# Floor, squares and head factors of four mLSTM heads: f32 column sums and a spread through memory in place of a weighted sum and diagonals

## The chip, the cores and the metric

The kernel runs on one core of a Trainium2 chip. A core has a matrix engine (TensorE, PE in the profile), three engines for elementwise work (VectorE, DVE; ScalarE, ACT; GpSimd, POOL) and one that issues transfers (SyncE, SP). POOL issues transfers as well. The metric is the device time of one execution in microseconds; a time given for a kernel is the median of its runs.

## The reference

Two layers over 512 tokens with 1024 channels. The first (layer A) mixes tokens by an mLSTM matrix memory with 4 heads of 192 channels beside a cross-attention to 256 memory tokens with 4 heads of 64, the second by a banded attention with 12 heads beside another cross-attention. Each has an output projection and a gated convolutional feed-forward part. What the change touches is the end of an mLSTM head:

```
h  = num / maximum(abs(den), exp(-m))
hm = h * rsqrt(mean(h*h over the 192 channels of the head) + EPS)
mix = hm * a_head_g * sigmoid(o)
```

`num` is the weighted sum of the values, `den` the sum of the weights, `m` the running maximum of the exponents. Since `h` is `num` over a number per token and head, the two steps are one factor per token and head: the product of `num` with `rsqrt(mean(num*num) + EPS * max(den*den, exp(-2m)))`. This is what the kernel computes.

## The kernel before, in words

Activations stand with channels on the 128 partitions and the 512 tokens along the free axis, in tiles of 128x512. A product of two f32 matrices is done by `mm3` (L167 to L171) as three products of a high and a low part: high by high (L169), high by low (L170), low by high (L171). `split` makes the two parts, the high one by a copy on ACT (L130), the low one by a difference on DVE (L131). Weights come by SP's queue into `wr` and are split into `wh` and `wl`.

In layer A the work of PE comes from two sources. A *job*, which is a generator, makes the parts that depend on one another: `mlstm_head(h)` for heads 0 to 3, and `memory_attention` for pairs of memory heads. A *filler* makes matmuls of projections and of the output projection, which wait for little. `weave(job, filler, each)` takes so many units of filler (a unit is one `mm3`) for each step of the job; `yield n` in a job stands for n steps. The order is: head 0, head 1, memory attention 0, head 2, memory attention 1, head 3. Filler for the first four is the input projection of later tiles; for memory attention 1 and head 3 it is the output projection. The order in which instructions come to an engine is then settled by a scheduler that works from the program, except where `pin` keeps an instruction at its place.

A head (`mlstm_head`) makes the weighted scores of four blocks of tokens (exponents are read to all partitions from memory into the tile `bias`, L1029; ACT's Exp at L1155, POOL's mask at L1157, the product at L1166), then multiplies them with the values (`products`), into two tiles `nums`. The first has 128 channels of the head. The second has the other 64 on one half of its partitions, and on the other half the denominator, the same in every row. The end of a head before the change:

- ACT squares both tiles (L1193), and DVE multiplies the numerators by the gate `og` (L1195).
- For each of 4 blocks of 128 tokens two f32 products (L1200, L1201) with the small constant matrix `mcf` give two columns per block: the sum of the squared numerators, and the mean of the squared denominator rows. Behind each block stands a yield of 0.581.
- DVE takes the maximum of the second column and `floor2`, scales it and adds the first column (L1205 to L1207). `rsqrt` (L213 to L222) is done by an integer start and three iterations on 128x4 elements.
- `diagonal` (L224 to L237) splits the factor and multiplies two copies of the identity by it (L231); after a yield of 2.673, `spread` (L240 to L245) multiplies a matrix of ones by the two diagonals (L244), so that each partition holds the factor of every token.
- DVE multiplies the gated numerators by it (L1214) and they are split into `mixes`, the operands of the output projection.

`floor2` is the bound `exp(-2m)`. Its row `mr` (4 heads x 512 tokens) is made in `gate_rows`, transposed in four parts by PE (L1097) into tokens x heads, and passed through Exp (L1099).

`OutProjection.part(g, *ks)` adds the products of input tiles ks to the output tiles of group g: group 0 is output tiles 0 to 2, group 1 is 3 and 4. `finish` makes those output tiles that are in no group (5 to 7 before) with `project`, adds each tile to the residual `xT`, and collects the squares for the next norm.

Of the kernel before, what the change touches and what calls it, by code (L numbers as in the profile page):

```python
# [9 lines left out]
F32 = mybir.dt.float32  # L10
# [3 lines left out]
ALU = mybir.AluOpType  # L14
# [9 lines left out]
AH = 4  # L24
# [31 lines left out]
def trunk(  # L56
# [30 lines left out]
    def sb(tag, shape, dtype=F32):  # L87
        count[0] += 1
        return pool.tile(shape, dtype, tag=tag, name=f"{tag}{count[0]}", bufs=bufs[tag])
# [23 lines left out]
    eps = cpool.tile([P, 1], F32, name="eps")  # L113
    V.memset(eps, EPS)

    mcf = cpool.tile([P, 3, 2], F32, name="mcf")
    V.memset(mcf, 0.0)
    V.memset(mcf[:, 0, 0:1], 1.0)
    V.memset(mcf[:HD, 1, 0:1], 1.0)
    V.memset(mcf[HD:, 1, 1:2], 1.0 / HD)  # L120
    V.memset(mcf[:HD, 2, 1:2], 1.0 / HD)
    V.memset(mcf[HD:, 2, 0:1], 1.0)


    HEADS = (slice(0, HD), slice(HD, P))

    pin = tc.keep_in_program_order
# [32 lines left out]
    def weights(*args):  # L160
        return parts(load(*args))

    def rows(w, c0, n, k0=0, k1=None):
        k1 = k1 if k1 is not None else w.shape[0] // P
        return w[k0 * P : k1 * P, c0 : c0 + n].rearrange("(k p) c -> p k c", p=P)
# [4 lines left out]
        nc.tensor.matmul(o, lh, rl, start=False, stop=False, skip_group_check=more)  # L170
        nc.tensor.matmul(o, ll, rh, start=False, stop=last, skip_group_check=more)  # L171

    def project(w, c0, act, tag="mm"):


        n = len(act)
        wh, wl = weights(rows(w, c0, P), n, P)
        o = ps(tag)
        for k in range(n):
            mm3(o, wh[:, k, :], wl[:, k, :], act[k][0], act[k][1], k == 0, k == n - 1)  # L180
            yield
        return o

    def run(gen):
        while True:
            try:
                next(gen)
            except StopIteration as end:
                return end.value
# [57 lines left out]
    def logarithms():  # L247

        pin(A.preload_act_table_set("natural_log_exp_and_others"))
# [357 lines left out]
    class OutProjection:  # L607
# [18 lines left out]

        def finish(self, gnames):
            logarithms()
            norm = Norm()
            acts = [[] for _ in gnames]  # L630
            for j in range(KT):
                o = self.o[j] if j in self.o else run(project(self.w, j * P, self.mixes))
                V.tensor_add(xT[j], xT[j], o)
                pin(G.dma_start(xspill[j], xT[j]))
                norm.add(xT[j])
                for a, g in zip(acts, gnames):
                    a.append(scaled(xT[j], g[:, j : j + 1]))
            return norm, acts
# [373 lines left out]
    e, u, c, r = (cpool.tile([P, TT, AH], F32, name=f"gate{i}") for i in range(4))  # L1012
    tot = cpool.tile([AH, 16], F32, name="tot")
    acol = cpool.tile([P, TT, AH], F32, name="acol")
    floor2 = cpool.tile([P, TT, AH], F32, name="floor2")
    NEXT = 4
    RO = [0, 512, 896, 1152, 1280]

# [12 lines left out]
    def gate_rows():  # L1031
# [58 lines left out]
            spread_exponents(i)  # L1090
        pin(V.tensor_tensor(out=mr, in0=mr, in1=br, op=ALU.add))
        V.tensor_scalar(mr, mr, -40.0, None, op0=ALU.max)
        yield
        tp = ps("tr")
        for T in range(TT):
            nc.tensor.transpose(tp[:, T * AH : (T + 1) * AH], ar[:, T * P : (T + 1) * P], ident[:AH, :AH])
            nc.tensor.transpose(tp[:, 16 + T * AH : 16 + (T + 1) * AH], mr[:, T * P : (T + 1) * P], ident[:AH, :AH])  # L1097
        pin(V.tensor_copy(acol, tp[:, :16].rearrange("p (t h) -> p t h", t=TT)))
        A.activation(floor2, tp[:, 16:32].rearrange("p (t h) -> p t h", t=TT), AF.Exp, scale=-2.0)  # L1099

    mixes = [None] * KT

# [41 lines left out]
    def mlstm_head(h):  # L1144
# [43 lines left out]
        yield from products(2)  # L1188
        yield from products(3)
        sqs = []  # L1190
        for o, j, r in ((nums[0], full, slice(0, P)), (nums[1], sh, rs)):
            sq = sb("t", [P, S])
            A.activation(sq, o, AF.Square)  # L1193
            sqs.append(sq)
            V.tensor_tensor(out=og[j][r, :], in0=o[r, :], in1=og[j][r, :], op=ALU.mult)  # L1195
        yield
        st = ps("sc")
        for T in range(TT):
            sl = slice(T * P, (T + 1) * P)
            nc.tensor.matmul(st[:, 2 * T : 2 * T + 2], sqs[0][:, sl], mcf[:, 0, :], start=True, stop=False)  # L1200
            nc.tensor.matmul(st[:, 2 * T : 2 * T + 2], sqs[1][:, sl], mcf[:, 1 + odd, :], start=False, stop=True)  # L1201
            yield 0.581
        st = st[:, : 2 * TT].rearrange("p (t c) -> p t c", c=2)
        z, fc = small(), small()
        V.tensor_tensor(out=z, in0=st[:, :, 1], in1=floor2[:, :, h], op=ALU.max)  # L1205
        V.tensor_scalar(z, z, EPS, 1e-35, op0=ALU.mult, op1=ALU.max)
        V.scalar_tensor_tensor(z, st[:, :, 0], 1.0 / DH, z, op0=ALU.mult, op1=ALU.add)  # L1207
        rsqrt(fc, z)
        dg = diagonal(fc)
        yield 2.673  # L1210
        fb = spread(dg, "sc")
        yield
        for j, r in ((full, slice(0, P)), (sh, rs)):
            V.tensor_tensor(out=og[j][r, :], in0=fb[r, :], in1=og[j][r, :], op=ALU.mult)  # L1214
            if mixes[j] is None:
                mixes[j] = sb("u", [P, S], F32R), sb("u", [P, S], F32R)
            split(mixes[j][0][r, :], mixes[j][1][r, :], og[j][r, :])

    outp = OutProjection(a_w_out, mixes, (0, 3, "mm"), (3, 5, "tr"))
    run(value_columns(1))  # L1220
    load_vectors(1)
    load_vectors(2)
# [16 lines left out]
    job = mlstm_head(3)  # L1239
    fill = chain(fill, outp.part(0, 7))  # L1240
    weave(islice(job, 13), fill, 0.85)
    fill = chain(fill, outp.part(1, 0, 1, 2, 6), outp.part(1, 3, 7))
    weave(job, fill, 0.862)
    run(chain(fill, outp.part(0, 4, 5), outp.part(1, 4, 5)))
    norm, (act,) = outp.finish([col["gffn"][:, 0:8]])


# [275 lines left out]
```

## Time and profile before

| | |
|---|---|
| runs | 1195.31, 1196.02, 1194.69 us; median 1195.31 |
| profiled execution | 1195.72 us |
| its span, first to last instruction | 1194.0 us |
| mean granted TensorE clock | 0.999 |
| busy PE, DVE, ACT, POOL | 99%, 81%, 61%, 11% |

The page of the profile gives the busy time of each engine, the clock in 40 slices of the span, the chain of work that ended last, and groups of instructions by line. A row of a timeline is: start in us, duration, engine, line, operation, output tile <- input tiles, shape, and in square brackets the engine's idle time ahead of it with what ended it. In a group, "x32 | 5.8, 251" means 32 records, 5.8 us busy, 251 ns mean. Matmuls overlap, so the price of one is the distance from its start to the next one's start. SPq and POOLq are the queues of transfers that SP and POOL issue.

### The profile page before, as it was taken

The page shows a single profiled execution, that of the slowest core. Times are in us where ns is not written, and L with a number is a line of the kernel's source. Part 1 is how long each engine was busy: PE and PEld are TensorE (multiplying, and loading weights), DVE is VectorE, ACT ScalarE, POOL GpSimd, SP SyncE. Part 2 cuts the span into 40 slices and gives each one's busy share as a digit, 9 for nine tenths or more (in the row PEclk, how much of TensorE's full clock was granted, in tenths as well). Part 3 has the DMA queues.
Part 4 walks back from the last instruction along what each step waited for, and adds up shares of the span by engine and source line. Part 5 has one row for each costly group of instructions (what it writes and reads, how often), then busy time and mean ns, then how long its engine had stood idle before and what let it go on. Part 6 is the DMA issues. An engine that isn't in the chain of part 4 may idle for free.

```text
span 1194.0 us, 18184 instructions
## 1 busy us (share of the span) xinstructions
PE 1183.5 (99%) x6719; PEld 1037.0 (87%) x6719; DVE 961.7 (81%) x1760; ACT 725.2 (61%) x1294; POOL 130.3 (11%) x222
## 2 busy tenths in 40 slices
PE   9999999999999999999999999999999999999997
PEld 9988888888899998999888888888889988999986
DVE  6877788788978888888698888997896888888855
ACT  5648677655656555555576677776565655555545
POOL 1211201010021111111020000101001011011100
PEclk9999999999999999999999999999999999999999
DMA  8645313444265676665464313246336455665551
GB/s 289 212 108 140 84 54 80 152 144 141 88 156 147 156 165 165 154 144 123 142 204 123 89 54 101 69 135 185 111 99 141 116 139 135 142 141 139 119 158 71
DMA packets 200155, 158.61 MB, mean 133 GB/s; under 512 B 8344, under 2 KB 179838, under 8 KB 200066
## 3 DMA queue, kind: packets, MB, share of 16 engines
q1 hardware_dynamic: 183906, 119.74, 34.1%
q0 software_dynamic: 15584, 36.67, 14.9%
q8 instruction: 53, 0.87, 0.3%
q10 hardware_dynamic: 576, 1.05, 0.2%
q14 instruction: 36, 0.29, 0.1%
HBM read 128.89 MB, written 32.46 MB: 135 GB/s over the span
## 4 chain that ended last, share of the span: by engine, by line
PE 92%; ACT 3%; DVE 2%; DMA 1%; SPq 1%; issue 0%; POOL 0%; POOLq 0%; DVEq 0%; ACTq 0%
PE pmm L169 15%; PE pmm L170 15%; PE pmm L171 15%; PE ptr L171 6%; PE ptr L169 6%; PE ptr L170 6%; PE pmm L785 6%; PE psc L171 5%; PE psc L170 5%; PE psc L169 5%; PE pmm L784 3%; PE psc L519 2%; PE ptr L1350 1%; DMA wr<-in_mem_w_kv_dram 1%; PE ptr L1371 1%; PE ptr L1372 1%
## 5 line engine op out<-in xcount | busy, mean ns | idle before, releaser
L169 PE MATMUL pmm<-u,wh 128*128 128x512 f32 (+1 forms) x872 | 309.1, 355 | 0.3 <-ACT u L130 0.2
L170 PE MATMUL pmm<-u,wh 128*128 128x512 f32 (+1 forms) x872 | 306.2, 351 | 0.0
L171 PE MATMUL pmm<-u,wl 128*128 128x512 f32 (+1 forms) x872 | 306.0, 351 | 0.0
L131 DVE TENSOR_TENSOR wl<-wr,wh 128x1024 fp32r<-128x1024 f32 (+3 forms) x172 | 199.8, 1163 | 57.0 <-ACT wh L130 55.0
L130 ACT CAST wh<-wr 128x1024 fp32r<-128x1024 f32 (+3 forms) x172 | 172.4, 1004 | 97.7 <-PE pmm L170 44.5
L171 PEld LDWEIGHTS pmm<-u,wl 128*128 128x128 f32 x872 | 164.5, 189 | 21.1
L169 PEld LDWEIGHTS pmm<-u,wh 128*128 128x128 f32 x872 | 164.5, 189 | 18.5 <-ACT u L130 1.1
L170 PEld LDWEIGHTS pmm<-u,wh 128*128 128x128 f32 x872 | 164.7, 189 | 18.2 <-DVE u L131 0.5
L169 PE MATMUL ptr<-u,wh 128*128 128x512 f32 x272 | 106.7, 392 | 0.0
L171 PE MATMUL ptr<-u,wl 128*128 128x512 f32 x272 | 106.1, 390 | 0.0
L753 POOL DMA_DIRECT2D xspill<-t x64 | 55.6, 869 | 461.1 <-ACT t L752 450.4
L170 PE MATMUL ptr<-u,wh 128*128 128x512 f32 x272 | 105.9, 389 | 0.0
L130 ACT CAST u<-pt 128x512 fp32r<-128x512 f32 x102 | 63.0, 620 | 46.8 <-DVE pt L875 46.7
L131 DVE TENSOR_TENSOR u<-pt,u 128x512 fp32r<-128x512 f32 x102 | 69.9, 688 | 11.2 <-ACT u L130 8.5
L169 PE MATMUL psc<-u,wh 128*128 128x256 f32 (+1 forms) x232 | 76.1, 328 | 0.0
L171 PE MATMUL psc<-u,wl 128*128 128x256 f32 (+1 forms) x232 | 75.9, 327 | 0.0
L170 PE MATMUL psc<-u,wh 128*128 128x256 f32 (+1 forms) x232 | 75.9, 327 | 0.0
L937 ACT ACTIVATE t<-t 128x512 f32<-128x512 f32 x34 | 21.6, 634 | 79.3 <-DVE t L660 79.3
L785 PE MATMUL pmm<-u,u 128*128 128x512 f32 x192 | 69.6, 397 | 0.0
L821 DVE TENSOR_TENSOR t<-t,pmm 128x256 f32<-128x256 f32 x72 | 30.2, 419 | 44.9 <-ACT t L819 44.8
L752 ACT COPY t<-ptr 128x512 f32<-128x512 f32 x64 | 37.4, 585 | 43.1 <-PE ptr L171 43.1
L660 DVE SCALAR_TENSOR_TENSOR t<-t,cols,t 128x511 f32<-128x511 f32 x80 | 59.7, 746 | 3.7 <-ACT t L667 3.7
(300 smaller groups left out, 2673.8 us busy)
## 6 DMA issues: line engine op xcount, KB each, us to landing
wr<-in_ffn_w_up_dram SPq DMA_DIRECT2D x54, 512.0 KB, 4.2
wr<-in_ffn_w_down_dram SPq DMA_DIRECT2D x38, 512.0 KB, 4.1
pt<-in_ffn_w_up_dram SPq DMA_DIRECT2D x34, 512.0 KB, 6.2
xspill<-t POOLq DMA_DIRECT2D x64, 256.0 KB, 5.2
wr<-in_a_w_in_dram SPq DMA_DIRECT2D x20, 512.0 KB, 3.7
xspill<-u POOLq DMA_DIRECT2D x32, 256.0 KB, 2.6
u<-xspill SPq DMA_DIRECT2D x32, 256.0 KB, 5.0
wr<-in_w_kv_dram SPq DMA_DIRECT2D x12, 512.0 KB, 3.7
```

Source lines behind the costliest of these rows:

```text
L130: high = A.copy(hi, src) if on_act else V.tensor_copy(hi, src)
L131: low = V.tensor_tensor(out=lo, in0=src, in1=f(hi), op=ALU.subtract)
L169: nc.tensor.matmul(o, lh, rh, start=first, stop=False, skip_group_check=more)
L170: nc.tensor.matmul(o, lh, rl, start=False, stop=False, skip_group_check=more)
L171: nc.tensor.matmul(o, ll, rh, start=False, stop=last, skip_group_check=more)
L519: nc.tensor.matmul(o, a, b, start=first and i == 0, stop=i == 1)
L660: V.scalar_tensor_tensor(acc[:, n:], src[:, : S - n], self.fw[:, c * FT + j : c * FT + j + 1], acc[:, n:], op0=ALU.mult, op1=ALU.add,)
L752: A.copy(t, o)
L753: G.dma_start(xspill[j], t, accum_op=ALU.add)
L784: nc.tensor.matmul(r[:, :H], w[1][:, k], p[i - 1][:, :H], start=False, stop=False, skip_group_check=True)
L785: nc.tensor.matmul(r, w[0][:, k], p[i - 1], start=False, stop=k == n - 1, skip_group_check=True)
L821: V.tensor_tensor(out=o, in0=o, in1=r[:, H:], op=ALU.add)
```

## The change

The bound becomes a row that is passed through Exp before it leaves its 4 partitions, scaled, and written to memory; from there it is read into two tiles, each holding the bound of two heads on 64 partitions each. In a head the squares of the second tile are bounded on the half with the denominator by one operation, and the two squared tiles are added. One f32 product per block with a column of ones then gives the whole sum (the scale takes account of the fact that the denominator stands in 64 rows). Heads 0 to 2 write the factor to memory and read it back to all partitions by POOL's queue, with a yield of 5.2; head 3 keeps the diagonals, with a yield of 4.2. The output projection gets a third group, output tile 5, and its `finish` loads the weights of the first two tiles left before it starts.

```diff
-    mcf = cpool.tile([P, 3, 2], F32, name="mcf")
...
-    def project(w, c0, act, tag="mm"):
+    def project(w, c0, act, tag="mm", ready=None):
...
-        wh, wl = weights(rows(w, c0, P), n, P)
+        wh, wl = ready or weights(rows(w, c0, P), n, P)
...
             logarithms()
+            rest = [j for j in range(KT) if j not in self.o]
+            ready = {j: weights(rows(self.w, j * P, P), KT, P) for j in rest[:2]}
             norm = Norm()
...
-                o = self.o[j] if j in self.o else run(project(self.w, j * P, self.mixes))
+                o = self.o[j] if j in self.o else run(project(self.w, j * P, self.mixes, ready=ready.get(j)))
...
-    floor2 = cpool.tile([P, TT, AH], F32, name="floor2")
+    floor2 = dram.tile([AH, S], F32, name="floor2")
+    floors = []
+    factors = dram.tile([AH, S], F32, name="factors")
...
+        A.activation(mr, mr, AF.Exp, scale=-2.0)
+        V.tensor_scalar(mr, mr, EPS * DH / HD, 1e-35, op0=ALU.mult, op1=ALU.max)
+        G.dma_start(floor2, mr)
+        for hp in range(2):
+            floors.append(sb("u", [P, S]))
+            for odd, half in enumerate(reversed(HEADS)):
+                row = floor2[2 * hp + odd]
+                src = bass.AP(tensor=row.tensor, offset=row.offset, ap=[[0, HD], [1, S]])
+                G.dma_start(floors[hp][half, :], src)
         yield
         tp = ps("tr")
         for T in range(TT):
             nc.tensor.transpose(tp[:, T * AH : (T + 1) * AH], ar[:, T * P : (T + 1) * P], ident[:AH, :AH])
-            nc.tensor.transpose(tp[:, 16 + T * AH : 16 + (T + 1) * AH], mr[:, T * P : (T + 1) * P], ident[:AH, :AH])
         pin(V.tensor_copy(acol, tp[:, :16].rearrange("p (t h) -> p t h", t=TT)))
-        A.activation(floor2, tp[:, 16:32].rearrange("p (t h) -> p t h", t=TT), AF.Exp, scale=-2.0)
...
         sqs = []
+        for o in reversed(nums):
+            sqs.insert(0, sb("t", [P, S]))
+            A.activation(sqs[0], o, AF.Square)
+        dr = HEADS[1 - odd]
+        V.scalar_tensor_tensor(
+            sqs[1][dr, :], sqs[1][dr, :], EPS * DH / HD, floors[hp][dr, :], op0=ALU.mult, op1=ALU.max
+        )
+        V.tensor_add(sqs[0], sqs[0], sqs[1])
         for o, j, r in ((nums[0], full, slice(0, P)), (nums[1], sh, rs)):
-            sq = sb("t", [P, S])
-            A.activation(sq, o, AF.Square)
-            sqs.append(sq)
             V.tensor_tensor(out=og[j][r, :], in0=o[r, :], in1=og[j][r, :], op=ALU.mult)
         yield
+        yield 3.6
         st = ps("sc")
         for T in range(TT):
-            sl = slice(T * P, (T + 1) * P)
-            nc.tensor.matmul(st[:, 2 * T : 2 * T + 2], sqs[0][:, sl], mcf[:, 0, :], start=True, stop=False)
-            nc.tensor.matmul(st[:, 2 * T : 2 * T + 2], sqs[1][:, sl], mcf[:, 1 + odd, :], start=False, stop=True)
-            yield 0.581
-        st = st[:, : 2 * TT].rearrange("p (t c) -> p t c", c=2)
+            nc.tensor.matmul(st[:, T : T + 1], sqs[0][:, T * P : (T + 1) * P], ones[:, :1], start=True, stop=True)
         z, fc = small(), small()
-        V.tensor_tensor(out=z, in0=st[:, :, 1], in1=floor2[:, :, h], op=ALU.max)
-        V.tensor_scalar(z, z, EPS, 1e-35, op0=ALU.mult, op1=ALU.max)
-        V.scalar_tensor_tensor(z, st[:, :, 0], 1.0 / DH, z, op0=ALU.mult, op1=ALU.add)
+        V.tensor_scalar(z, st[:, :TT], 1.0 / DH, None, op0=ALU.mult)
         rsqrt(fc, z)
-        dg = diagonal(fc)
-        yield 2.673
-        fb = spread(dg, "sc")
-        yield
+        if h < AH - 1:
+            pin(G.dma_start(factors[h].rearrange("(t p) -> p t", p=P), fc))
+            fb = sb("rb", [P, S])
+            pin(G.dma_start(fb, bass.AP(tensor=factors.tensor, offset=factors[h].offset, ap=[[0, P], [1, S]])))
+            yield 5.2
+        else:
+            dg = diagonal(fc)
+            yield 4.2
+            fb = spread(dg, "sc")
+            yield
...
-    outp = OutProjection(a_w_out, mixes, (0, 3, "mm"), (3, 5, "tr"))
+    outp = OutProjection(a_w_out, mixes, (0, 3, "mm"), (3, 5, "tr"), (5, 6, "sc"))
...
-    fill = chain(fill, outp.part(1, 0, 1, 2, 6), outp.part(1, 3, 7))
+    fill = chain(fill, outp.part(2, 0, 1, 2, 3, 6, 7), outp.part(1, 0, 1, 2, 6), outp.part(1, 3, 7))
     weave(job, fill, 0.862)
-    run(chain(fill, outp.part(0, 4, 5), outp.part(1, 4, 5)))
+    run(chain(fill, outp.part(0, 4, 5), outp.part(1, 4, 5), outp.part(2, 4, 5)))
```

In the kernel after the change, lines behind the constants stand 9 lines earlier (L169 to L171 become L160 to L162); the bounding operation is L1197, the addition L1200, the column sums L1207, the write and the read of the factor L1212 and L1214, the multiplication by the factor L1222.

More of the change, by code (lines that the diff above doesn't have):

```diff
@@ L114, in trunk @@
     V.memset(eps, EPS)
-    mcf = cpool.tile([P, 3, 2], F32, name="mcf")
[L117 to L122, printed above, removed]
     HEADS = (slice(0, HD), slice(HD, P))
```

## The prediction, made before the change was run

> **What bounds the kernel now.** I read the page first: the busy line, the granted clock, and the chain of work that ended last.
>
> ```profile
> span 1194.0 us, 18184 instructions
> ...
> PE 1183.5 (99%) x6719; PEld 1037.0 (87%) x6719; DVE 961.7 (81%) x1760; ACT 725.2 (61%) x1294; POOL 130.3 (11%) x222
> ...
> PEclk9999999999999999999999999999999999999999
> ...
> PE 92%; ACT 3%; DVE 2%; DMA 1%; SPq 1%; issue 0%; POOL 0%; POOLq 0%; DVEq 0%; ACTq 0%
> ```
>
> PE is busy for 99% of the span, its clock is never held back, and 92% of the chain is PE. So two things count: how many steps PE has to do, and where it stands still. What DVE, ACT and POOL do is free as long as its result is there when PE comes to the instruction that reads it. PE's price per step I took from the timeline, in an undisturbed stretch of projection:
>
> ```profile
> 164.83 0.40 PE L170 MATMUL pmm<-u,wh 128*128 128x512 f32 x1
> ...
> 170.29 0.39 PE L170 MATMUL pmm<-u,wh 128*128 128x512 f32 x1
> ```
>
> The second row is 24 instructions after the first: 5.46 / 24 = 0.2275 us for a 128x512 product. The 0.39 or 0.40 in a row is the pipelined duration; the step from start to start is what a product costs.
>
> The sum below is made against the profiled execution, 1195.72 us with a span of 1194.0. The median of the runs shown, 1195.31, lies 0.41 lower.
>
> **What is removed: steps of PE.** Sums of squares first. The groups say how many products there are, the timeline of PE in head 3 what they cost.
>
> ```profile
> L1201 PE MATMUL psc<-mcf,t 128*128 128x2 f32 x32 | 5.8, 251 | 0.0
> ```
> ```profile
> 241.49 0.28 PE L1200 MATMUL psc<-mcf,t 128*128 128x2 f32 x2
> ...
> 242.30 0.49 PE L169 MATMUL ptr<-u,wh 128*128 128x512 f32 x1
> 242.62 0.40 PE L170 MATMUL ptr<-u,wh 128*128 128x512 f32 x1
> ```
>
> Each of these f32 products leaves two records, so L1201 has 16 products in the four heads, and L1200 as many. Four of them take 242.30 - 241.49 = 0.81 us, and the full product behind them takes 0.32 instead of 0.23: 0.9 for four, 0.225 each. The new sum has 4 products per head instead of 8, so 16 go: **-3.6**. The new ones have one output column instead of two. Two columns cost as much here as 512 do in the other type, so the price doesn't follow the columns and I keep it; if it halved after all, the 16 that stay would give 1.8 more.
>
> The floor row is no longer transposed (L1097), four products less:
>
> ```profile
> 88.75 0.20 PE L1096 MATMUL ptr<-ident,t 4*128 4x4 f32 x1
> 88.81 0.20 PE L1097 MATMUL ptr<-ident,t 4*128 4x4 f32 x1
> ```
>
> A step of 0.06 each: **-0.25**. And heads 0 to 2 lose two spreading products (L244) each: 6 x 0.2275 = **-1.37**. Together -5.2 us.
>
> PE also stands still at places that the change rewrites. The timeline of PE at head 2's spread, at head 2's memory attention, at head 3's first weighted product, and at head 3's end:
>
> ```profile
> 212.61 0.39 PE L171 MATMUL pmm<-u,wl 128*128 128x512 f32 x1
> 212.91 0.50 PE L244 MATMUL psc<-t,onesr 128*128 128x512 f32 x1
> 213.25 0.40 PE L169 MATMUL pmm<-u,wh 128*128 128x512 f32 x1
> 213.51 0.50 PE L244 MATMUL psc<-t,onesr 128*128 128x512 f32 x1
> 213.85 0.39 PE L170 MATMUL pmm<-u,wh 128*128 128x512 f32 x1
> ```
> ```profile
> 233.04 0.28 PE L170 MATMUL psc<-u,u 128*128 128x128 f32 x1
> 233.47 0.73 PE L169 MATMUL ptr<-pt,u 128*128 128x512 f32 x2 [0.16 <-ACT pt L130]
> 234.04 0.22 PE L171 MATMUL psc<-u,u 128*128 128x128 f32 x1
> 234.35 0.50 PE L170 MATMUL ptr<-pt,u 128*128 128x512 f32 x1
> ```
> ```profile
> 186.66 0.39 PE L169 MATMUL pmm<-u,wh 128*128 128x512 f32 x1
> 187.12 0.73 PE L519 MATMUL psc<-u,u 128*128 128x512 f32 x2
> ```
> ```profile
> 251.75 0.39 PE L171 MATMUL ptr<-u,wl 128*128 128x512 f32 x1
> 252.30 0.73 PE L169 MATMUL pmm<-u,wh 128*128 128x512 f32 x2 [0.16 <-ACT u L130]
> ```
>
> Four steps from 212.61 to 213.85 take 1.24 instead of 0.91: 0.33 of waiting. Against their normal step the rows after 233.04 and 234.04 come 0.3 and 0.2 late, 187.12 comes 0.23 late, 252.30 comes 0.32 late. I count **-1.4** for all of them; what is late in their place is counted anew below. That is -6.6 so far.
>
> **What is added: a round trip through memory.** In heads 0 to 2 POOL writes the factor (512 separate elements of four bytes, L1212 after the change) and then reads it back to all partitions (256 KB, L1214). No row shows a write like this one. The nearest are the DMA view's, of the same queue, and the landing line of the tile "bias":
>
> ```profile
> bias<-exponents POOLq DMA_DIRECT2D x4, 256.0 KB, 3.7
> ...
> exponents<-t POOLq DMA_DIRECT2D x1, 8.0 KB, 2.8
> ...
> exponents<-t POOLq DMA_DIRECT2D x1, 2.0 KB, 1.5
> ```
> ```profile
> DMA to landing us min/median/max: 2.9/3.6/7.7
> ```
>
> Lower end: the 2 KB write, 1.5, and the fastest read, 2.9: 4.4. Upper end: 2.8 and the slowest read, 7.7: 10.5. I take 2.4 for the write (same size as the 1.5, but in far smaller pieces, so towards 2.8) and the median 3.6 for the read: a trip of **6.0**. The Trainium skill ("DMA: Bandwidth & Descriptors", Specifications) says that below 512 B a transfer becomes a read-modify-write; no row here shows writes that short, and if it bites, the long-trip rival below is the case.
>
> What waits for the trip: L1222 (the multiplication by the factor) stands on DVE in program order, and what is queued behind it on DVE waits too; PE waits when it comes to a product that needs any of it.
>
> *Head 2* costs most, because memory attention 1 and then head 3 stand behind it. Before, on DVE:
>
> ```profile
> 207.45 0.16 DVE L1205 TENSOR_TENSOR s<-psc,floor 128x4 f32<-128x4 f32 x1 [1.06 <-PE psc L1201]
> ...
> 212.17 1.29 DVE L231 TENSOR_TENSOR t<-ident,s 128x512 fp32r<-128x512 f32 x2
> 214.05 1.28 DVE L1214 TENSOR_TENSOR u<-psc,u 128x512 f32<-128x512 f32 x2 [0.59 <-PE psc L244]
> ```
>
> The sums end at about 207.2, and PE starts head 3's first weighted product (233.47 above) 26.2 us later. In that stretch PE waited 0.66 (the 0.33 of the spread and the 0.3 before 233.47), and in the changed order it has five 512-wide products less (the two spreads, and three of filler that go elsewhere): 26.2 - 0.66 - 5 x 0.2275 = 24.4 us of work. From L1214 to 233.47 the other chain took 19.4: multiply, split, the query scaling, softmax, transposes, values, head 3's scores, its split. In the changed order one weight split of 0.6 moves ahead of the multiplication and runs during the trip: 18.8. Ahead of it stand the sums' arrival (0.25), the operations up to the factor (from 207.45 to 212.17 before, 4.7 us for 14 small and three longer ones; the changed order has two small ones and one of 0.5 less, so 3.8), the trip 6.0, and 0.1 to start: 0.25 + 3.8 + 6.0 + 0.1 + 18.8 = 29.0. PE therefore waits 29.0 - 24.4 = **+4.6**, and every microsecond of the trip counts in full; the break-even is a trip of 1.4. Part of the wait comes even earlier, because the output projection's filler needs head 2's tile itself.
>
> *Head 1*: seven long DVE operations stand between its small ones, so the factor is ready 5.4 us after the sums; 6.0 for the trip and 5.7 for the multiplications, the split and memory attention 0's first reductions make 17.1, where the changed order gives PE 16.5 us of work: **+0.6**, break-even 5.4.
>
> *Head 0*: factor ready after 3.2, then 6.0, two multiplications and the split of head 1's first weighted scores, which is queued behind them (some 2.4): 11.6 against 11.5 us of work on PE (55 instructions): **+0.1**, break-even 5.9.
>
> **What is hidden.** The floors' own trip (a write and four reads) starts about where the transposes stood (88.75) and is first needed at head 0's sums, a whole head later. The bounding operation and the addition on DVE (some 0.7 us each) and the squares come ahead of the sums, covered by 3.6 more units of filler; without the cover each head would lose 1.4. Head 3 keeps its diagonals, with 4.2 units of filler ahead of the spread instead of 2.7, for the sum's filler stands earlier now; I take **+0.1**. The write and read of head 2 on POOL's queue stand ahead of the clearing of memory attention 1's query tiles, which has 2 us of room. SP's queue gets seven loads more because the weights are cut differently, at a DMA load of some 0.6; they are prefetched, so nothing.
>
> **The end of the output projection.** Three column groups are now done as filler, so two projections (16.4 - 5.5 = 10.9 us) instead of three cover the additions and norm sums of the tiles. PE's total work is the same. DVE's room there, by the view of windows:
>
> ```profile
> 255.40:280.00 24.60, 24.60 (x111) 20.35 (x110) 21.33 (x29) 15.03 (x22) 4.36 (x8) 1.00 0.64 200
> ```
>
> The third figure pair is DVE: 21.33 busy in 24.60, 3.3 us free. Cutting 5.5 of cover could cost up to 2.2; but the weight splits of the first two projections are moved forward out of it. Between 0 and 2.2 I take **+0.3**.
>
> **Sum.** -5.2 - 1.4 + 4.6 + 0.6 + 0.1 + 0.1 + 0.3 = -0.9, so 1194.8 in a profiled execution and **1194.4** as a median. The change saves PE about 6.6 us and hands 5.7 of them back as waiting.
>
> **Rivals.**
>
> *Short trip.* The write is as quick as the 2 KB one and the read near the fastest, 4.65 in all. Then heads 0 and 1 wait for nothing and head 2 waits 3.25: -6.6 + 3.25 + 0.4 = -2.95, 1192.4. For the chain of 18.8 I assumed that all of it is late by the full delay; in the window 218 to 233.5 DVE was idle for part of the time, waiting for PE, and if some 1.8 of such waiting closes up, it is 1190.5. I price the case at 1191.4. For it: the DMA queues are lightly used around the heads, and DVE's rows show idle time. Against: the median of the read is 3.6. The Trainium skill ("DMA: Bandwidth & Descriptors", Anatomy of one DMA, SWDGE path) fits 2.0 us plus bytes over 436e3; as an estimate that is 2.0 for the write and 2.6 for the read, 4.6, and by it this rival's time. The trace's 1.5 for 2 KB and 3.7 for 256 KB differ from it in both directions.
>
> *Long trip: slower than before.* 512 four-byte pieces are slow to write, or the read queues behind other traffic as the 7.7 did. At a trip of 8.0 head 2 waits 6.6, head 1 2.6, head 0 2.1: -6.6 + 11.3 + 0.4 = +5.1, 1200.4. From a trip of 6.3 on the change gains nothing, from 7.1 it is slower by over 0.2%. For it: no row shows such a write. Against: 8 KB in 2.8.
>
> *DVE late in the end of the projection.* With the trip as forecast, between the 2.2 above and the whole 5.5 of lost cover is waited for: 1196.3 to 1199.6, priced at 1197.9.
>
> *It doesn't do what it says*: the one-column products cost more than 0.225, for instance. Weight loads of the same size speak against it, and it would only move the sum within the range.
>
> **How the numbers follow.** Forecast (1192.5 to 1196.5): 0.45. Short trip (1190.4 to 1192.4): 0.35. Long trip: 0.12. DVE late: 0.08. About 0.2%, 2.4 us, is what a measurement of this kernel can tell from no change, so the bounds are 1192.9 and 1197.7. Faster: the short trip and 0.05 of the forecast, 0.40. Slower: the long trip and half of the late DVE, 0.16. The same: what is left, 0.44. The range goes from the short trip's lower end, 1190.5, to 1199.0, about a trip of 7.5; what is left out is half of the long trip and a little below.
>
> **What would show it.** PE has 16 + 6 + 4 products less. In head 2 L1212 and L1214 land 6 us after the last rsqrt step, DVE's multiplication waits for DMA, and PE has waits of 4 to 5 us in sum between the output projection's product with head 2's tile and head 3's first weighted product; under 1 us in sum at heads 0 and 1. If the trip is 4.5 or the wait at head 3 is below 3, the short trip holds; if L1212 alone takes 4 or more, the long one. I would be wrong altogether if the wait showed up in the convolution or the second layer, where no instruction changed, or if PE's step changed.

## The result, and the profile after

| | before | after |
|---|---|---|
| median | 1194.91 us (5 runs, 1194.57 to 1196.02) | 1236.84 us (5 runs, 1233.58 to 1240.21) |
| ratio | | 1.0349, 95% interval 1.0338 to 1.0360 |
| profiled execution, span | 1195.72, 1194.0 | 1240.21, 1238.5 |
| mean granted TensorE clock | 0.999 | 0.981 |

The change makes the kernel 3.5% slower, 44.5 us by the two profiled spans. The forecast was 1194.4, with a range that ended at 1199.0, and a rival for which a long trip through memory made it slower, at 1200.4. The direction of that rival is what came, at eight times its size. The page of the profile after, the lines that answer to those shown of before:

```profile
span 1238.5 us, 18111 instructions
...
PE 1191.0 (96%) x6677; PEld 1040.0 (84%) x6677; DVE 961.6 (78%) x1744; ACT 722.1 (58%) x1293; POOL 136.0 (11%) x233
...
PE   9999796959999999999999999999999999999997
...
PEclk9999888979999999999999999999999999999999
...
PE 82%; DVE 6%; DMA 5%; ACT 4%; issue 3%; POOL 0%; SPq 0%; ACTq 0%; DVEq 0%; POOLq 0%
```

A slice is 31 us. PE's row falls to 7, 6 and 5 in the fifth, seventh and ninth, between 124 and 279 us, and in the same stretch the clock's row, all nines before, falls to 8 and 7. Behind 279 us both are as they were. PE's share of the chain went from 92% to 82%, and what came in is DVE, DMA and ACT. (PE's busy time is larger after, although PE has fewer products: the record of a product is longer at half the clock, 0.63 in place of 0.39 in the rows below.)

The view of waits says where, what PE waited for, how often and how long at most:

```profile
PE pmm L160 <- ACT u L121: 11.4, 1, 11.4
PE psc L510 <- ACT t L567: 10.0, 2, 9.9
PE ptr L161 <- DVE pt L122: 9.9, 1, 9.9
PE ptr L160 <- ACT pt L121: 2.6, 2, 1.9
```

Three waits of ten microseconds, one for each trip, and one of 1.9 in head 0 before any trip. ACT and DVE are named, but they only pass the delay on. The timeline of DVE in head 0 shows whom they wait for:

```profile
153.97 1.28 DVE L1222 TENSOR_TENSOR u<-rb,u 128x512 f32<-128x512 f32 x2 [10.33 <-DMA rb<-factors]
155.18 0.68 DVE L122 TENSOR_TENSOR pt<-t,pt 128x512 fp32r<-128x512 f32 x1
```

DVE stands 10.33 us in front of the multiplication, and head 1's split, queued behind it, is what PE needs. POOL's timeline and the DMA view give the trip's two legs (the last figure of a DMA row is the time from issue to landing):

```profile
136.77 0.79 POOL L1212 DMA_DIRECT2D factors<-s  x1 [4.21 <-DVE s L213]
147.56 0.54 POOL L1214 DMA_DIRECT2D rb<-factors  x1 [10.00 <-DMA factors<-s]
```
```profile
rb<-factors POOLq DMA_DIRECT2D x3, 256.0 KB, 6.4
...
factors<-s POOLq DMA_DIRECT2D x3, 2.0 KB, 9.8
```

The write of 2 KB takes 9.8 us, the read 6.4; I had put 2.4 and 3.6. And behind each wait PE itself is slow, as its timeline in head 1's first products shows:

```profile
145.59 0.39 PE L160 MATMUL ptr<-pt,u 128*128 128x512 f32 x1
155.91 0.79 PE L161 MATMUL ptr<-pt,u 128*128 128x512 f32 x1 [9.93 <-DVE pt L122]
156.50 0.63 PE L162 MATMUL ptr<-pt,u 128*128 128x512 f32 x1
156.93 0.63 PE L160 MATMUL ptr<-pt,u 128*128 128x512 f32 x1
...
161.19 0.45 PE L161 MATMUL pmm<-u,wh 128*128 128x512 f32 x1
161.48 0.40 PE L162 MATMUL pmm<-u,wl 128*128 128x512 f32 x1
```

Before the wait a product takes 0.2275, from 156.50 on 0.427, and at 161.2 the full rate is back. The windows view, over the five stretches at half rate, the first of them and the sum (the column behind POOL is the clock):

```profile
123.60:130.30 6.70, 6.70 (x19) 5.40 (x20) 5.24 (x9) 5.14 (x8) 0.51 (x2) 0.51 0.01 2
...
sum 25.10, PE 25.00 PEld 20.47 DVE 19.89 ACT 18.44 POOL 1.15; mean PE 5.00 PEld 4.09 DVE 3.98 ACT 3.69 POOL 0.23
```

So the 44.5 us divide up. Between starts of products, above the normal step, the trace holds gaps of 10.1, 10.0 and 11.6 at the three trips, 2.05 in head 0 before them, and 1.15 and 1.16 later (in memory attention 1 at 273 us, in the feed-forward part at 362): 36.0 in sum. 25.1 us of work at 0.427 in place of 0.2275 cost 25.1 x (1 - 0.2275 / 0.427) = 11.7. Less the 5.2 of products removed that makes 42.5; the last 2 are smaller waits, the longest 0.84.

### The profile page after: what moved, and what is told of

Same layout as the page of the kernel before. It is cut to its first block, busy times and chain, and to the rows that moved or that the text cites. A ratio compares the mean times of both kernels' runs of the same rounds, so it can differ in the third digit from the quotient of the medians.

```text
span 1238.5 us, 18111 instructions
## 1 busy us (share of the span) xinstructions
PE 1191.0 (96%) x6677; PEld 1040.0 (84%) x6677; DVE 961.6 (78%) x1744; ACT 722.1 (58%) x1293; POOL 136.0 (11%) x233
## 4 chain that ended last, share of the span: by engine, by line
PE 82%; DVE 6%; DMA 5%; ACT 4%; issue 3%; POOL 0%; SPq 0%; ACTq 0%; DVEq 0%; POOLq 0%
PE pmm L160 12%; PE pmm L161 12%; PE pmm L162 12%; PE ptr L161 6%; PE ptr L160 6%; PE ptr L162 6%; PE pmm L778 5%; PE psc L162 5%; PE psc L160 5%; PE psc L161 5%; PE pmm L777 3%; PE psc L510 2%; DMA rb<-factors 2%; PE ptr L1358 1%; DVE wl L122 1%
## 5 line engine op out<-in xcount | busy, mean ns | idle before, releaser
L160 PE MATMUL pmm<-u,wh 128*128 128x512 f32 (+1 forms) x864 | 308.4, 357 | 11.5 <-ACT u L121 11.4
L162 PE MATMUL pmm<-u,wl 128*128 128x512 f32 (+1 forms) x864 | 305.3, 354 | 1.0 <-DVE wl L122 1.0
L122 DVE TENSOR_TENSOR wl<-wr,wh 128x1024 fp32r<-128x1024 f32 (+5 forms) x173 | 199.8, 1157 | 66.2 <-ACT wh L121 64.4
L121 ACT CAST wh<-wr 128x1024 fp32r<-128x1024 f32 (+5 forms) x173 | 172.0, 997 | 104.4 <-PE pmm L161 45.8
L160 PEld LDWEIGHTS pmm<-u,wh 128*128 128x128 f32 x864 | 164.8, 191 | 30.5 <-ACT u L121 12.3
L162 PEld LDWEIGHTS pmm<-u,wl 128*128 128x128 f32 x864 | 164.3, 190 | 22.6 <-DVE wl L122 1.4
L160 PE MATMUL ptr<-u,wh 128*128 128x512 f32 x272 | 106.5, 392 | 0.0
L162 PE MATMUL ptr<-u,wl 128*128 128x512 f32 x272 | 106.1, 390 | 0.0
L160 PE MATMUL psc<-u,wh 128*128 128x256 f32 (+1 forms) x240 | 79.7, 332 | 0.0
L162 PE MATMUL psc<-u,wl 128*128 128x256 f32 (+1 forms) x240 | 79.2, 330 | 0.5 <-DVE wl L122 0.5
L161 PE MATMUL psc<-u,wh 128*128 128x256 f32 (+1 forms) x240 | 79.0, 329 | 0.0
```

The costliest lines, as they stand in the source:

```text
L121: high = A.copy(hi, src) if on_act else V.tensor_copy(hi, src)
L122: low = V.tensor_tensor(out=lo, in0=src, in1=f(hi), op=ALU.subtract)
L160: nc.tensor.matmul(o, lh, rh, start=first, stop=False, skip_group_check=more)
```

## The experiments

The theory after reading the two traces: the write is slow because of its 4-byte pieces, and all the rest follows. The rivals: a trip by this queue is always that slow, or the rest of the change (floors, sums, third group) costs too.

### Without the trip: e1_diag, e10_sums, e9_group

```diff
-        if h < AH - 1:
+        if False:
```

> All four heads spread their factor by diagonals and two products, as head 3 does; all else as in the changed kernel (no write, no read back of factors). Theory (the round trip through memory is the whole loss): the three waits of 10 to 12 us and the half-rate stretches behind them go, what stays is the saving of sums and transposes, 1190 to 1193 us. Rival (the rest of the change, that is the third group of the output projection, the new order and the floors' trip, carries part of the loss): 1200 or more, with a PE wait of over 2 us that stays.

1196.87 us median (10 runs, 1195.15 to 1200.04), ratio to before 1.0011 (1.0000 to 1.0021). In the profiled execution the three waits and all half-rate stretches are gone, so the trips are the loss. But the gain that I expected with them gone isn't there: the time lies between the two ranges. The view of waits names one reason:

```profile
PE ptr L160 <- ACT pt L121: 1.6, 1, 1.6
...
PE psc L235 <- DVE t L222: 0.4, 2, 0.2
```

The first is the one of head 0, at 121 us: a cast of the last weighted scores stands on ACT behind a SiLU, whose chain begins with a weight load that lands late. Gaps above the normal step between 80 and 460 us are 8.1 us here and 3.9 before: 4.2 more, against the 3.85 of PE's steps that this kernel saves (5.2 without the 1.37 of the spreads, which are back).

e10_sums also takes back the third group and the early weights:

```diff
-    outp = OutProjection(a_w_out, mixes, (0, 3, "mm"), (3, 5, "tr"), (5, 6, "sc"))
+    outp = OutProjection(a_w_out, mixes, (0, 3, "mm"), (3, 5, "tr"))
```

> e1_diag without the third group of the output projection and without the early weights: before, with only the new floor row, the added squares and the column sums (and the new yields). Theory (in e1_diag PE's saving of 3.85 us is eaten mainly by a wait of 2 us in head 0, where a late weight load stands ahead of the cast of the last weighted scores, and by smaller waits; all of it from the new order in the first heads): the wait near 121 us stays, and the time is within 1.5 us of e1_diag and of before. Rival (the third group eats the saving, since two projections cover less than three): 1191 to 1193.

1197.48 (9 runs, 1196.28 to 1199.76), ratio 1.0023 (1.0013 to 1.0033). This is 0.6 above e1_diag, as expected, but 2.6 above the kernel before (1194.90 beside it), where at most 1.5 was expected. The wait at 121 us stays, so it belongs to the floors, sums and new yields; no run separates these. e9_group has only the third group and the early weights, put into the kernel before:

> The kernel before with only the third group of the output projection and the early weights of its end. Theory (this part is nearly neutral: PE does the same products, and what the early weights save at the end is given back by two late weight splits there): within 1.5 us of before. Rival (it is a gain of its own that the rest of the change hides): 1191 to 1193.

1194.85 (11 runs), ratio 0.9996 (0.9988 to 1.0005): neutral, as expected, and my term of +0.3 for this part lies within the interval. Its trace has no gap of over 0.25 us between 255 and 460 us, so the late splits of the expectation are not there.

### What is slow about the write: e2_row, e3_16b, e4_sp

e2_row makes the factor a row ahead of the write, e3_16b writes four neighbouring values at once and multiplies in that order, e4_sp changes the queue.

```diff
# e2_row
-            pin(G.dma_start(factors[h].rearrange("(t p) -> p t", p=P), fc))
+            fr = st[:TT, P : 2 * P]
+            nc.tensor.transpose(fr, fc, ident)
+            frs = sb("t", [P, S])[:TT, :P]
+            V.tensor_copy(frs, fr)
+            pin(G.dma_start(factors[h].rearrange("(t p) -> t p", p=P), frs))
# e3_16b (the multiplication's matching views are left out here)
+            pin(G.dma_start(factors[h].rearrange("(p t) -> p t", p=P), fc))
# e4_sp
+            pin(nc.sync.dma_start(factors[h].rearrange("(t p) -> p t", p=P), fc))
```

> The factor is transposed by one product into 4 rows and written as 4 pieces of 512 bytes in place of 512 pieces of 4 bytes; read back as in the changed kernel. Theory (the small pieces are what is slow): the write lands in 1.5 to 2 us in place of 9.8, the trip with the transposition is 6 to 8, and the time comes near the recorded forecast, 1193 to 1200. Rival (a trip by this queue is slow whatever is written): the write stays near 10 us and the time near 1237.

> The factor is written in the order partition, block: 128 pieces of 16 bytes; the multiplication reads the spread row in the matching order. Theory (a price for each piece, one after the other: 9.8 less 1.6 over 512 is 16 ns): 1.6 + 128 x 0.016 = 3.7 us for the write, PE waits of about 2 to 3 us less than half of those of the changed kernel, 1198 to 1208. Rival (a price by bytes or by the queue): write near 10, time near 1237.

> The changed kernel with the write of the factor issued by SP's queue in place of POOL's; the read stays on POOL's. Theory (the write is slow in memory, whoever issues it): it lands after 8 to 10 us, PE waits as in the changed kernel, 1225 to 1245. Rival (POOL's queue is what is slow): the write lands in under 3 us and the time is 1198 to 1206, like e2_row and e3_16b.

The DMA views of the three, in that order:

```profile
rb<-factors POOLq DMA_DIRECT2D x3, 256.0 KB, 3.7
factors<-t POOLq DMA_DIRECT2D x3, 2.0 KB, 1.6
```
```profile
rb<-factors POOLq DMA_DIRECT2D x3, 256.0 KB, 4.5
...
factors<-s POOLq DMA_DIRECT2D x3, 2.0 KB, 1.7
```
```profile
rb<-factors POOLq DMA_DIRECT2D x3, 256.0 KB, 6.4
...
factors<-s SPq DMA_DIRECT2D x3, 2.0 KB, 9.1
```

Times: e2_row 1203.65 (ratio 1.0073, 1.0057 to 1.0089), e3_16b 1201.95 (1.0059, 1.0044 to 1.0074), e4_sp 1232.50 (1.0312, 1.0287 to 1.0338). The same 2 KB by the same queue take 1.6 or 1.7 us when the pieces are larger, and by another queue the small ones take 9.1. So the queue is not the cause; but my price of 16 ns a piece falls too, for 128 pieces of 16 bytes should then have taken 3.7. The read behind the slow write is slow too: 6.4 behind the small pieces, 3.7 and 4.5 behind the large ones. What slows it isn't shown; in head 0 of the changed kernel four reads of exponents and SP's transfers run beside it.

With the write repaired the trip is about what I had put it at, and the waits are nearly what I forecast. Yet the times are 9.3 (e2_row) and 7.6 (e3_16b) above the forecast, and e2_row misses the 1193 to 1200 that I expected. The PE timeline of e3_16b at head 2 shows one reason:

```profile
220.44 0.39 PE L162 MATMUL pmm<-u,wl 128*128 128x512 f32 x1
222.44 0.50 PE L160 MATMUL pmm<-u,wh 128*128 128x512 f32 x1 [1.61 <-ACT u L121]
223.35 0.50 PE L161 MATMUL pmm<-u,wh 128*128 128x512 f32 x1 [0.41 <-DVE u L122]
...
225.71 0.63 PE L162 MATMUL pmm<-u,wl 128*128 128x512 f32 x1
```

Even a wait of 1.8 followed by some shorter ones is followed by half-rate products (0.63 in place of 0.39). The other reason is head 0's 1.8 us, which no trip causes.

### What makes pieces slow: e6_pieces, e7_places, e11_spacing

All three spread by diagonals and write, in heads 0 to 2, something that nothing reads, each head another way: e6_pieces and e7_places as their expectations say, e11_spacing the 512 values of 4 bytes into every second, fourth and eighth element.

```diff
# e11_spacing
+            if h < AH - 1:
+                pin(G.dma_start((by8, by16, by32)[h][:, 0].rearrange("(t p) -> p t", p=P), fc))
```

> Spread by diagonals in all heads, and one write per head that nothing reads: head 0 writes 512 pieces of 4 bytes, each 512 bytes from the next; head 1 writes 256 pieces of 8 bytes side by side; head 2 writes 128 pieces of 4 bytes side by side. In e5_unread 512 pieces of 4 bytes side by side took 8.2 to 9.7 us, in e3_16b 128 pieces of 16 bytes took 1.7 to 2.2, so a price of 16 ns for any piece is out. Theory (small pieces that fall into the same stretch of memory are written one after the other, by how many share it): head 0 under 3 us, head 1 about 4 to 5, head 2 about 3 to 4. Rival (each piece under 16 bytes costs about 16 ns wherever it lies): 9 to 10, 5 to 6, 3 to 4. Second rival (the count of pieces of one transfer, past some 128): 9 to 10, 3 to 6, 1.7.

> Spread by diagonals in all heads, and writes that nothing reads: head 0 copies its factor by four transfers of 128 pieces of 4 bytes to another on-chip tile instead of memory; head 1 writes 512 pieces of 4 bytes, 64 bytes apart; head 2 writes 512 pieces of 4 bytes side by side by SP's queue in place of POOL's. Theory (memory writes small pieces of one stretch one after the other): head 0 under 2.5 us each, head 1 under 4, head 2 8 to 10. Rival (the queue or its making of the pieces is slow): head 0 3 to 4 each, head 1 9 to 10, head 2 under 3.

> Spread by diagonals; each of heads 0 to 2 writes 512 pieces of 4 bytes that nothing reads, 8, 16 and 32 bytes apart. So far: side by side (16 in 64 bytes) 8 to 11 us, 64 bytes apart 2.2, 512 bytes apart 2.3; 8-byte pieces side by side 3.6, 16-byte pieces 1.7. Theory (what counts is how many pieces fall into one stretch of 64 bytes, each waiting for the one before): 8 bytes apart 3.5 to 5, 16 apart 2 to 3, 32 apart 2 to 2.5. Rival (the size of a piece counts, if it isn't alone in a far longer stretch, as 512 bytes): 8 to 10 at 8 and 16 bytes, and still over 4 at 32.

Rows of the DMA views, of e6_pieces (512 bytes apart; pairs; 128 pieces), of e7_places (on chip; 64 bytes apart; SP's queue), of e11_spacing (8, 16, 32 bytes apart):

```profile
apart<-s POOLq DMA_DIRECT2D x1, 2.0 KB, 2.3
...
pairs<-s POOLq DMA_DIRECT2D x1, 2.0 KB, 3.6
...
few<-s POOLq DMA_DIRECT2D x1, 0.5 KB, 7.7
```
```profile
onchip<-s POOLq DMA_DIRECT2D x4, 0.5 KB, 1.9
...
lines<-s POOLq DMA_DIRECT2D x1, 2.0 KB, 2.2
...
factors<-s SPq DMA_DIRECT2D x1, 2.0 KB, 11.0
```
```profile
by<-s POOLq DMA_DIRECT2D x1, 2.0 KB, 3.7
...
by<-s POOLq DMA_DIRECT2D x1, 2.0 KB, 2.3
...
by<-s POOLq DMA_DIRECT2D x1, 2.0 KB, 2.4
```

| pieces | within 64 bytes | us |
|---|---|---|
| 512 of 4 bytes, side by side | 16 | 8.2 to 11.0 |
| 128 of 4 bytes, side by side | 16 | 7.7 |
| 512 of 4 bytes, 8 bytes apart | 8 | 3.7 |
| 256 of 8 bytes, side by side | 8 | 3.6 |
| 512 of 4 bytes, 16 bytes apart | 4 | 2.3 |
| 128 of 16 bytes, side by side | 4 | 1.7 |
| 512 of 4 bytes, 32, 64 or 512 bytes apart | 2, 1, 1 | 2.4, 2.2, 2.3 |
| 4 x 128 of 4 bytes, on chip | | 1.9 each |

Neither the number of pieces nor their size decides, and not the queue: a quarter of the pieces, side by side, take nearly as long as all, and 512 pieces apart from one another take 2.3. What orders the whole table is how closely the pieces lie in memory, steeply above four in 64 bytes. The 64 is a ruler and not a finding: all pieces are evenly spaced, and the distance from the start of one to the next (4 bytes, 8, 16 and more) orders the table as well. The row of 128 pieces is one that I had wrong: my theory and the rivals gave it 1.7 to 4 us. Only the write to memory is slow, not the one on chip. That the memory takes such pieces one after the other is the reading that fits; the runs don't show it inside the memory. The Trainium skill ("DMA: Bandwidth & Descriptors", Specifications) has a read-modify-write below 512 bytes; the runs agree that short pieces can be slow, but not that all are, for 4-byte pieces 16 bytes apart took no more than 2.3.

### What the write does to others: e5_unread

```diff
             dg = diagonal(fc)
+            if h < AH - 1:
+                pin(G.dma_start(factors[h].rearrange("(t p) -> p t", p=P), fc))
```

> Spread by diagonals in all heads as in e1_diag, but heads 0 to 2 also write their factor in 512 pieces of 4 bytes, which nothing reads and nothing waits for but the end. Theory (the write also holds up the transfers of the other queues while it lasts): weight loads issued during the write land in 8 to 14 us instead of 3.7, and the time is 2 to 10 us above e1_diag. Rival (only the trip itself costs): the same as e1_diag within 1 us.

1196.03 (10 runs), ratio 1.0011 (1.0001 to 1.0020), as e1_diag; the rival held. The write did delay others: the DMA view between 212 and 235 us has eight reads of "xspill" beside it, first in this kernel, then in the one before.

```profile
u<-xspill SPq DMA_DIRECT2D x8, 256.0 KB, 8.9
```
```profile
u<-xspill SPq DMA_DIRECT2D x8, 256.0 KB, 4.9
```

They land 4 us later (e1_diag, without the write, has 5.2), so the theory was right that other transfers are held up, but nothing waits for these. In the changed kernel weight loads beside the write landed up to 14.6 us after their issue, but the chain that ended last goes through the factor's read at all three trips. A delayed transfer is a cost only if it ends a wait.

### One trip alone: e15_one

```diff
-        if h < AH - 1:
+        if h == 1:
```

> The changed kernel with the trip through memory in head 1 alone, diagonals in heads 0, 2 and 3. Theory (each trip makes PE wait for about its length less its break-even, and then half-rate steps follow until the clock is granted again): one wait of 9 to 11 us, some 10 to 25 steps at 0.427 us behind it worth 2 to 4 us, 1206 to 1211 in all, 11 to 14 above e1_diag. Rival (the clock record costs nothing beyond the wait): 9 to 10 above e1_diag.

1205.93 (4 runs, 1205.58 to 1207.44), ratio 1.0091 (1.0078 to 1.0105): 9.1 above e1_diag's median. PE's timeline:

```profile
173.28 0.39 PE L162 MATMUL pmm<-u,wl 128*128 128x512 f32 x1
182.80 1.22 PE L510 MATMUL psc<-u,u 128*128 128x256 f32 x4 [9.14 <-ACT t L567]
183.82 0.63 PE L160 MATMUL pmm<-u,wh 128*128 128x512 f32 x1
...
187.23 0.42 PE L161 MATMUL pmm<-u,wh 128*128 128x512 f32 x1
```

The wait is 9.3 above the step, and from 182.8 to 187.2 PE runs at half rate, which by the same formula costs 4.4 x 0.467 = 2.1. By the spans of the two profiled executions, 1204.5 and 1194.3, the trip costs 10.2; two spread products (0.46) and head 1's small waits go with it (e1_diag has 0.57 and more there), so 9.3 + 2.1 less 1.0 is 10.4. The wait and the cost behind it lie in the ranges that the theory gave, but their sum does not: it left out what goes with the trip, and 9.1 by the medians is under its 11 to 14 and within the rival's 9 to 10. It is the step of the products in the trace, not the time, that shows the second cost.

### Can the saving be had: e12_early, e13_cover, e16_cover6

All are without the trip, and all have more filler ahead of the spreads of heads 0 to 2 (4.9 units, e16_cover6 6.0). Beside that e12_early is to read the exponents' rows earlier, and e13_cover and e16_cover6 give head 0 more filler.

```diff
# e12_early
-    NEXT = 4
+    NEXT = 5
# e13_cover
-    weave(mlstm_head(0), fill, 1.4)
+    weave(mlstm_head(0), fill, 1.6)
# e12_early, e13_cover (e16_cover6: 6.0)
-            yield 4.2
+            yield 4.9 if h < AH - 1 else 4.2
```

> e1_diag with the exponents' rows read five ahead in place of four, and 4.9 units of filler in place of 4.2 ahead of the spread in heads 0 to 2. Theory (the wait of 2 us near 121 us comes from a weight load that starts beside the read of an exponents row and lands in 6 us instead of under 4; read earlier, they part): the wait goes, and the waits of 0.35 at the spreads of heads 0 and 2; 1192.5 to 1194.5, below before. Rival (the load is late for another reason): the wait stays and only 0.7 goes, 1195 to 1196.

> e1_diag with 1.6 units of filler per step of head 0 in place of 1.4, and 4.9 units ahead of the spreads of heads 0 to 2. Theory (the last weighted scores of head 0 are cast 2 us after PE wants them; more filler ahead of them covers it): the wait near 121 us shrinks to under 0.5, and the time is 1192.5 to 1195. Rival (the filler taken forward is missing in heads 1 and 2 and opens waits of the same size there): 1195.5 to 1198.

> e13_cover with 6.0 units of filler ahead of the spreads of heads 0 to 2 in place of 4.9. Theory (without the trips, every small wait that the new order opened can be covered by filler, and the 3.85 us that PE saves then show): the waits of 0.46 and 0.26 at the spreads go, 1191.5 to 1194, below before by 0.1 to 0.3%. Rival (filler taken there is missing at another place): 1194 to 1196, no better than e13_cover.

e12_early 1198.80 (ratio 1.0027, 1.0017 to 1.0037): the wait of head 0 stays at 1.8 us, and the time is above both ranges. The edit did not part the two transfers: POOL still issues a read of exponents at 109.62 us (109.68 in e1_diag), only the next, smaller row, and the weight load beside it lands after 6.1 us in place of 6.0. So why that load lands late is open, and the read beside it is not ruled out. e13_cover 1194.38 (11 runs, 1193.40 to 1196.63; ratio 0.9996, 0.9987 to 1.0005): the load is as late, but the wait shrinks to 0.4, and this is the best version, though not to be told from before. e16_cover6 1198.02 (1.0023, 1.0013 to 1.0033): here the rival's mechanism held, filler taken forward is missing later, and it cost 2 us more than the rival's range. Its view of waits:

```profile
PE psc L160 <- DVE t L1168: 2.6, 1, 2.6
```

A new wait of 2.6 us where head 3's scores start behind memory attention 1, with half-rate products behind it; it is longer than the waits that were to be covered. No version here beats the kernel before by more than the runs can tell.

## Why the prediction was wrong, step by step

- **PE's steps.** Right: 5.2 us are gone, and the balance above closes with it. The step outside the half-rate stretches is unchanged.
- **Waits that go (-1.4).** Wrong in sum: without the trips (e1_diag) there are 4.2 us more of gaps than before, where I had counted 1.4 less. I had followed the changed order at the heads' ends and not in head 0's middle, where the floors' work (one more Exp, one more scaling, five transfers) shifts what comes after. That it is this work is argued from its place ahead of the wait; no run has the floors alone.
- **The trip of 6.0.** This is the step that failed. "I take 2.4 for the write (same size as the 1.5, but in far smaller pieces, so towards 2.8)": measured 9.8. Both rows that I took as ends were writes in long pieces, so they bounded the size and said nothing of the pieces' place. The read, 3.6, came as 6.4 behind that write, and as 3.7 and 4.5 with the write repaired.
- **What the trip costs.** Right in form, measured with its true length. From issue of the write to DVE's start the trips of heads 0, 1 and 2 are 17.2, 15.8 and 17.2. Less my break-evens of 5.9, 5.4 and 1.4 that gives waits of 11.3, 10.4 and 15.8; the gaps measured are 10.1, 10.0 and, for head 2, 11.6 with 2.9 in memory attention 1 behind it.
- **The clock.** Missing altogether: in the trace of before the clock never falls, and I priced a wait as its own length. It is 11.7 us in all, and 2.1 beside a wait of 9.3 where it stands alone (e15_one).
- **The write beside others.** I had said nothing of it; it delays transfers, and in e5_unread that costs nothing.
- **The end of the projection (+0.3).** Not contradicted: with this part alone (e9_group) the time is between 1.4 us under and 0.6 over that of before. Two weight splits come 1.2 and 0.7 late in the changed kernel, at 363 and 370 us, but they stand in the convolutional feed-forward part, where I had said that no wait should show up; e9_group and e10_sums don't have them, e1_diag has one of 0.5, and their cause is open. It is not so either that no instruction of the second layer changed: both layers use the same `finish`, so the second one's projection loads two weights early as well.
- **The rivals.** "Long trip" named the cause ("no row shows such a write") and the place where it decides. Its chance of 0.12 was too small for an operation that no row shows, and its price too low: it was taken from a trip of 8.0, although the bounds above it went to 10.5. "If L1212 alone takes 4 or more, the long one": it took 9.8.

With 17 us in place of 6 and nothing else changed, my sum would have read -6.6 + 37.5 + 0.4 = +31, about 1227 instead of 1194. The rest is the clock and the waits outside the trips, head 0's above all.

## What to carry to other kernels

Before a tile with tokens on partitions is written to memory, look at the length of its pieces and at the distance from one to the next: 2 KB took 1.6 us as four rows and 9.8 as 512 neighbouring words, and turning the tile first or writing four words per partition avoids it. A trip that another engine waits for in order must be priced with its break-even, and an operation that no row shows deserves a wide range on its slow side, not the nearest row of the same size. A long wait of TensorE costs more than its length, because the products behind it run at half rate for some microseconds.

## What the runs showed of the hardware that was not expected

- Writes to memory with 16 pieces of 4 bytes in each 64 bytes took 8.2 to 11.0 us for 512 pieces and 7.7 for 128, with 8 pieces 3.6 or 3.7, with four or fewer 1.7 to 2.4. During such a write little moves; the view of DMA between 240 and 249.3 us of the changed kernel:

```profile
DMA  5544910000000990000000000906000600007100
...
DMA packets 431, 0.20 MB, mean 22 GB/s; under 512 B 79, under 2 KB 431, under 8 KB 431
...
q1 hardware_dynamic: 399, 0.20, 35.2%
q0 software_dynamic: 32, 0.00, 1.8%
```

  That is 22 GB/s against a mean of 129 over the span. POOL's queue (q0) has 32 packets with 1.8% of the engines' time, and all of them start within 0.4 us, 1.5 us after the issue; so the pieces are sent early and the wait is for their end. SP's queue (q1) has 35.2% of the engines' time for 0.20 MB: single packets of 1 KB take up to 8.2 us, so other transfers are held up meanwhile.

- After a wait of 9 to 12 us products ran at 0.427 us in place of 0.2275 for another 4 to 6 us. The Trainium skill ("TensorE: Matmul & The Clock Gate", Part 1) describes a gate that halves the clock after an idle window of some 3.4 us and gives 426.7 ns for a step of 512 columns then; the trace agrees with that step. It agrees with a window of that length too: all 68 changes of the clock in the 16 traces lie, within 3 ns, on a grid of 3.413 us, which starts elsewhere in each execution. It doesn't agree that the window has to be idle throughout: waits of 2.05 (head 0 of the changed kernel) and 1.83 (e10_sums) were followed by half-rate products too, while 1.77 and 1.85 (e1_diag, e5_unread) and 2.0 (e2_row) were not. What decides is how much of one stretch of the grid PE is busy. The windows view over two such stretches at head 0's wait, in the changed kernel and then in e5_unread (the second figure is PE's busy time, the column behind POOL the clock):

```profile
120.34:123.76 3.42, 1.53 (x7) 0.94 (x5) 1.36 (x4) 2.34 (x4) 0.00 (x0) 1.00 0.57 155
123.76:127.17 3.41, 3.41 (x11) 2.88 (x11) 2.02 (x4) 1.89 (x4) 0.00 (x0) 0.50 0.00 0
```
```profile
119.24:122.65 3.41, 2.41 (x14) 1.76 (x12) 1.99 (x4) 1.46 (x2) 0.47 (x2) 1.00 0.67 173
122.65:126.06 3.41, 2.72 (x14) 2.27 (x15) 1.90 (x4) 2.74 (x6) 0.00 (x0) 1.00 0.00 0
```

  In the first kernel the whole wait falls into one stretch, PE is busy for 1.53 us of it, and the next stretch runs at half rate; in the second the wait is split over two stretches and the clock stays. Over all traces, behind their first 10 us, a stretch with 1.53 us or less was always followed by half rate and one with over 2.1 never; between 1.67 and 2.1 both came. So a wait near 2 us costs the clock in one execution and not in the next: of the eight executions of e12_early one had a mean clock of 0.999 and took 1197.15 us, the others had 0.997 and took 1198.39 to 1199.87.
